# A seven-product FFN in layer 0 as well, and layer 1's conditioning dots in halves

## The chip, the cores and the metric

The kernel runs on one core of a Trainium2 chip. The metric is the device time of one execution in microseconds; the kernel before takes 2206.89 us (median of three runs, 2206.26 to 2207.37).

## What is computed

A trunk of two layers over 256 latent and 256 context tokens of width 1024. Each layer is a SwiGLU FFN of half weight, a token mixer (three kinds of attention, merged by gates) and a second such FFN. Every norm is modulated by a shift, a scale and a gate from a conditioning vector, one vector for the latent tokens and one for the context tokens. In layer 1 the context stream ends at the mixer.

```python
def _swiglu(h, w1, w3, w2):
    return (jax.nn.silu(h @ w1) * (h @ w3)) @ w2      # 1024 -> 2816 -> 1024

for l in range(DEPTH):                                # DEPTH = 2
    mx = jnp.split((sc_x @ ada_w[l] + ada_b[l])[:, None, :], N_MOD, axis=-1)   # N_MOD = 9
    mc = jnp.split(sc_c @ ada_w[l] + ada_b[l], N_MOD, axis=-1)
    x = x + mx[2] * 0.5 * _swiglu(_modulate(x, norm_gain[l, 0], mx[0], mx[1]), ...)
    xc = xc + mc[2] * 0.5 * _swiglu(...)
    y_x, y_c = _token_mixer(...)                      # with mx[3], mx[4], mc[3], mc[4]
    x = x + mx[5] * y_x
    x = x + mx[8] * 0.5 * _swiglu(_modulate(x, norm_gain[l, 2], mx[6], mx[7]), ...)
    if ctx_out:                                       # not in the last layer
        xc = xc + mc[5] * y_c
        xc = xc + mc[8] * 0.5 * _swiglu(...)
```

The conditioning vectors sc_x and sc_c go through a matrix of 1024 by 9216 for each layer. The kernel computes these nine modulation rows as dot products on VectorE: for each modulation m and each block k of 128 rows a load of 128 by 1024 (512 KB), and one dot with the vector of each stream that is needed.

## The kernel before

Activations lie with the features on the partitions, 512 tokens side by side (the first 256 latent, the other 256 context). Every weight and activation is split in two parts of a rounded format, hi and lo, and each product is three matmuls (`mm3`, L214 to L216): lo by hi, hi by lo, hi by hi. A weight unit is loaded by SP's queue, cast to hi on ScalarE and subtracted to lo on VectorE.

**A plain FFN** (the loop at L807) makes 22 tiles of 128 hidden features. A tile is two products with K = 1024 over 512 columns, a silu, a gate product, and a split into g. After groups of 8, 7 and 7 tiles comes an out phase: eight output blocks c, each accumulated over the group's tiles and added into x on VectorE. The layer's second FFN is (0, 1), the next layer's first is (1, 0).

**A seven-product FFN** (`ff_sevens`, L544), used for (1, 0) alone, takes two tiles as a 2 by 2 block matrix and saves one of eight block products. The token side uses combinations of the activations made once at the start (`token_forms`); the weight side is combined from the loaded blocks by two accumulating loads on GpSimd's queue (blocks n and s3) and two additions on VectorE (`preadd`, L594). The work is written out as a list of steps. For a pair p of tiles they are p2, p6, p5, p7, p1 of the next pair, p4, p3; each is 24 matmuls of 256 columns. After the pairs that end a group (6, 6 and 4 tiles; the last 6 are done by the ordinary out phase) come eight steps "out 0" to "out 7", each over the group's tiles with 512 columns. Out 0 leaves out the group's last two tiles; out 1 starts on the others, then does out 0's last two, then its own.

What a step's product needs is a form: the combined weight, cast by ScalarE to hi (L618) and subtracted by VectorE to lo (L627). There are four form buffers, so the form of step f + 4 is cast when step f is done. Loads go in the order of the steps through eight buffers of 128 by 1024 (`topup`, L578); a buffer is released when its form is made.

The order of ScalarE, VectorE, SP and GpSimd within `ff_sevens` is the written one (`manual_schedule`). After the matmuls of a step the loop writes: ScalarE's copy of the product's bank (s1, sv, sw or su; not in p2, p5 and p3), VectorE's low part of the previous gate result (L762), VectorE's sum with a second bank (p2, p7, p3) or, in an out step, the two additions into x (L722); then the cast and subtraction of form f + 4, and, in p2, p7, p4 and p3, the gate: silu on ScalarE, product on VectorE (L749), cast of g on ScalarE (L761). In p2, p7 and p3 the product is written behind the subtraction, in p4 ahead of it. The product banks q1 and q3 go on accumulating: p7 adds to q1 after ScalarE has copied sv, p4 after it has copied sw.

**The dots** of layer 1 (`ada`, L282) are a generator with two buffers of its own. In the plain FFN `hook` (L306) draws from it after every tile and out block; all 112 dots of layer 1 (five modulations for two streams, four for one) lie in (0, 1). Outside `ff_sevens` VectorE's order is set by a planner and not by the text.

Of the kernel before, what the change touches and what calls it, by code (L numbers as in the profile page):

```python
# [13 lines left out]
BF16 = mybir.dt.bfloat16  # L14
AF = mybir.ActivationFunctionType
ALU = mybir.AluOpType
# [4 lines left out]
KD = 8  # L21
# [9 lines left out]
STRASSEN = ((1, 0),)  # L31
# [47 lines left out]
class Builder:  # L79
# [6 lines left out]
    def __init__(self, ctx, tc, a):  # L86
# [21 lines left out]
        self.owed = 0.0  # L108

# [171 lines left out]

    def ada(self, l, mods, cond):  # L282
        nc, a = self.nc, self.a
        M, sm = self.mods[l], self.sm[l]
        self.araw = [self.qkv.tile([128, 1024], F32, tag="pair", name="araw") for _ in range(2)]
        for m in mods:
            ns = (0,) if l == DEPTH - 1 and m > 4 else (0, 1)
            for k in range(KD):
                raw = self.araw[k % 2]
                nc.sync.dma_start(raw, a["ada"][l, m, k])  # L290
                self.ada_dot(l, m, k, raw, cond, ns)
                if k < KD - 1:
                    yield len(ns)
            for s in ns:
                d = M[:, s, m, :]
                nc.vector.tensor_tensor(out=d, in0=d, in1=sm[:, SM_ADAB + m * KD:SM_ADAB + (m + 1) * KD], op=ALU.add)
                if m in (1, 4, 7):
                    j = m // 3
                    nc.vector.scalar_tensor_tensor(out=self.gs[l][:, s, j, :], in0=d, scalar=1.0,
                                                   in1=sm[:, SM_GAIN + j * KD:SM_GAIN + (j + 1) * KD],  # L300
                                                   op0=ALU.add, op1=ALU.mult)
                elif m in (2, 5, 8):
                    nc.vector.tensor_scalar_mul(d, d, 0.5)
            yield len(ns)
# [239 lines left out]
    def ff_sevens(self, l, i, banks, halves, gm):  # L544
# [20 lines left out]
        for p, k in steps:  # L565
# [3 lines left out]
            elif k in need:  # L569
                b = {"r0": (0, None), "r1": (1, None), "n": (2, 3), "s3": (0, 2), "r3": (3, None)}[need[k]]  # L570
                loads.append(((p, need[k]), W[p, b[0]], None if b[1] is None else W[p, b[1]], 1024))
        loads = deque(loads)
        free = deque(self.rawp.tile([128, 1024], F32, tag="raw", name="raw") for _ in range(4))
# [50 lines left out]
        def subs(new):  # L624
# [5 lines left out]
            preadd(state["nf"])  # L630
            topup()
# [133 lines left out]
        if pend[0]:  # L765
            pend[0]()
        return gts
# [829 lines left out]
    def build(self):  # L1597
# [8 lines left out]
        for l in range(DEPTH):  # L1606
# [10 lines left out]
                       lambda *v: self.start_norm(l, 2, acc2, *v), pre)  # L1617
            if not last:
                self.adaq = self.ada(l + 1, range(NMOD), self.cond(nc.scalar))
# [143 lines left out]
```

## Time and profile before

| | |
|---|---|
| median of 3 runs | 2206.89 us |
| profiled execution | 2206.14 us |
| its span, first to last instruction | 2204.4 us |
| TensorE busy | 2186.8 us, 99% |
| VectorE busy | 1543.9 us, 70% |
| ScalarE busy | 994.2 us, 45% |
| DMA, mean rate | 149 GB/s |
| granted TensorE clock | 0.999 |

In the rows PE is TensorE, PEld its weight load, DVE VectorE, ACT ScalarE, POOL GpSimd, SPq and POOLq the DMA queues of SyncE and GpSimd. Times are in microseconds from the start of the span, unless a mean in ns is named. A timeline's row is start, duration, engine, line, operation, written tile <- read tiles, shapes, count, and in brackets the idle time of the engine just before, with what ended it. Durations on VectorE, ScalarE and TensorE overlap the next instruction's start by some 0.1 us or more, so the cost in a full queue is read from start to start.

### The profile page before, as it was taken

The page shows a single profiled execution, that of the slowest core. Times are in us where ns is not written, and L with a number is a line of the kernel's source. Part 1 is how long each engine was busy: PE and PEld are TensorE (multiplying, and loading weights), DVE is VectorE, ACT ScalarE, POOL GpSimd, SP SyncE. Part 2 cuts the span into 40 slices and gives each one's busy share as a digit, 9 for nine tenths or more (in the row PEclk, how much of TensorE's full clock was granted, in tenths as well). Part 3 has the DMA queues.
Part 4 walks back from the last instruction along what each step waited for, and adds up shares of the span by engine and source line. Part 5 has one row for each costly group of instructions (what it writes and reads, how often), then busy time and mean ns, then how long its engine had stood idle before and what let it go on. Part 6 is the DMA issues. An engine that isn't in the chain of part 4 may idle for free.

```text
span 2204.4 us, 34597 instructions
## 1 busy us (share of the span) xinstructions
PE 2186.8 (99%) x12912; PEld 1901.0 (86%) x12912; DVE 1543.9 (70%) x3477; ACT 994.2 (45%) x2506; POOL 126.3 (6%) x162
## 2 busy tenths in 40 slices
PE   9999999999999999999999999999999999999998
PEld 6888888887888877888888899999998889889998
DVE  4787877759554455689787777666777776677665
ACT  4423233548443365433223345444554565565543
POOL 3000000101001000000000000000011101000000
PEclk9999999999999999999999999999999999999999
DMA  8565654222123212446568645654542233445553
GB/s 328 191 213 176 213 194 174 91 86 71 62 66 103 92 58 82 139 159 222 183 198 276 229 119 139 163 147 124 159 149 96 84 118 109 160 133 174 183 183 114
DMA packets 94808, 328.57 MB, mean 149 GB/s; under 512 B 10928, under 2 KB 11824, under 8 KB 94640
## 3 DMA queue, kind: packets, MB, share of 16 engines
q1 hardware_dynamic: 89280, 308.52, 42.5%
q0 software_dynamic: 4928, 16.78, 3.6%
q8 instruction: 102, 1.67, 0.3%
q10 hardware_dynamic: 432, 1.06, 0.2%
q14 instruction: 66, 0.54, 0.1%
HBM read 322.12 MB, written 4.19 MB: 148 GB/s over the span
## 4 chain that ended last, share of the span: by engine, by line
PE 85%; issue 9%; DVE 4%; ACT 1%; DMA 1%; POOL 0%; SPq 0%; POOLq 0%; DVEq 0%; ACTq 0%
PE mm L214 20%; PE mm L216 20%; PE mm L215 20%; PE s L215 5%; PE s L216 5%; PE s L214 5%; PE s L209 2%; PE o L209 2%; PE t L209 2%; PE t L1088 1%; DVE wlo L205 1%; DVE nm L1074 0%; PE t L865 0%; DVE wlo L627 0%; DVE P L1162 0%
## 5 line engine op out<-in xcount | busy, mean ns | idle before, releaser
L204 ACT CAST whi<-raw 128x256 fp32r<-128x256 f32 (+4 forms) x1246 | 463.6, 434 | 437.1 <-issue 197.1
L205 DVE TENSOR_TENSOR wlo<-raw,whi 128x256 fp32r<-128x256 f32 (+2 forms) x1238 | 508.2, 456 | 194.6 <-ACT whi L204 191.8
L214 PE MATMUL mm<-h,wlo 128*128 128x512 f32 (+2 forms) x1352 | 472.5, 349 | 0.0
L216 PE MATMUL mm<-h,whi 128*128 128x512 f32 (+2 forms) x1352 | 465.7, 344 | 0.0
L215 PE MATMUL mm<-h,whi 128*128 128x512 f32 (+2 forms) x1352 | 465.4, 344 | 0.0
L279 DVE SCALAR_TENSOR_TENSOR junk<-araw,cond 128x1024 bf16<-128x1024 f32 x224 | 270.9, 1219 | 22.8 <-DMA araw<-in_ada 22.4
L214 PEld LDWEIGHTS mm<-h,wlo 128*128 128x128 f32 (+1 forms) x1352 | 255.7, 189 | 35.2 <-issue 6.2
L216 PEld LDWEIGHTS mm<-h,whi 128*128 128x128 f32 (+1 forms) x1352 | 255.5, 189 | 31.4
L215 PEld LDWEIGHTS mm<-h,whi 128*128 128x128 f32 (+1 forms) x1352 | 255.8, 189 | 29.2 <-issue 0.2
L214 PE MATMUL mm<-g,wlo 128*128 128x512 f32 (+1 forms) x764 | 266.8, 349 | 0.0
L215 PE MATMUL mm<-g,whi 128*128 128x512 f32 (+1 forms) x764 | 265.9, 348 | 0.0
L216 PE MATMUL mm<-g,whi 128*128 128x512 f32 (+1 forms) x764 | 265.8, 348 | 0.0
L214 PE MATMUL s<-h,wlo 128*128 128x256 f32 (+1 forms) x768 | 252.2, 328 | 0.0
L215 PE MATMUL s<-h,whi 128*128 128x256 f32 (+1 forms) x768 | 252.2, 328 | 0.0
L216 PE MATMUL s<-h,whi 128*128 128x256 f32 (+1 forms) x768 | 252.1, 328 | 0.0
L214 PEld LDWEIGHTS mm<-g,wlo 128*128 128x128 f32 x764 | 144.6, 189 | 18.4
L215 PEld LDWEIGHTS mm<-g,whi 128*128 128x128 f32 x764 | 144.7, 189 | 18.2
L216 PEld LDWEIGHTS mm<-g,whi 128*128 128x128 f32 x764 | 144.6, 189 | 18.2
L215 PEld LDWEIGHTS s<-h,whi 128*128 128x128 f32 x768 | 146.0, 190 | 13.0
L214 PEld LDWEIGHTS s<-h,wlo 128*128 128x128 f32 x768 | 146.0, 190 | 13.0
L216 PEld LDWEIGHTS s<-h,whi 128*128 128x128 f32 x768 | 146.1, 190 | 12.8
L618 ACT CAST whi<-raw 128x1024 fp32r<-128x1024 f32 (+2 forms) x94 | 91.7, 975 | 93.3 <-PE mm L216 58.8
(304 smaller groups left out, 3345.4 us busy)
## 6 DMA issues: line engine op xcount, KB each, us to landing
raw<-in_w SPq DMA_DIRECT2D x130, 512.0 KB, 4.3
araw<-in_ada SPq DMA_DIRECT2D x128, 512.0 KB, 3.7
raw<-in_win SPq DMA_DIRECT2D x90, 512.0 KB, 3.3
raw<-in_w13p SPq DMA_DIRECT2D x50, 512.0 KB, 4.0
raw<-in_w2b SPq DMA_DIRECT2D x48, 448.0 KB, 3.9
raw<-in_w2a SPq DMA_DIRECT2D x24, 512.0 KB, 4.4
raw<-in_wbr SPq DMA_DIRECT2D x24, 512.0 KB, 3.3
raw<-in_w13p POOLq DMA_DIRECT2D x20, 512.0 KB, 5.6
```

The lines of the kernel that those rows point to most:

```text
L204: nc.scalar.copy(hi[:, c], raw[:, c])
L205: eng.tensor_tensor(out=lo[:, c], in0=raw[:, c], in1=hi[:, c].bitcast(F32), op=ALU.subtract)
L209: self.nc.tensor.matmul(out, lhsT=lhsT, rhs=rhs, start=start, stop=stop, **kw)
L214: nc.tensor.matmul(out, lhsT=sl, rhs=mh, start=start, stop=False, **kw)
L215: nc.tensor.matmul(out, lhsT=sh, rhs=ml, start=False, stop=False, **kw)
L216: nc.tensor.matmul(out, lhsT=sh, rhs=mh, start=False, stop=stop, **kw)
L279: self.nc.vector.scalar_tensor_tensor(out=junk, in0=raw, scalar=1.0, in1=cond[s], op0=ALU.mult, op1=ALU.mult, accum_out=self.mods[l][:, s, ...
L618: nc.scalar.copy(hi[:, :n], raws[key][:, :n])
L1088: nc.tensor.transpose(pt[:, b * 128:(b + 1) * 128], P[:, b * 128:(b + 1) * 128], self.ident)
```

## The change

The list `STRASSEN` of seven-product FFNs becomes (0, 1) and (1, 0). The norm ahead of (0, 1) keeps its results for the token forms (`stash`).

The dots of layer 1 leave the generator. `ff_sevens` puts their loads into its own list of loads, each behind the load of the step it is tied to, through the same eight buffers. In (0, 1) modulations 0, 1 and 2 are tied to the 24 out steps, one load of 512 KB each, for both streams. In (1, 0) modulations 3 and 4 (16 loads, both streams) are spread over the 24 out steps, and modulations 5, 6 and 7 (24 loads, latent stream only) over the 27 steps p1, p4 and p5 of the pairs after the first. When the form of such a step has been subtracted (in `subs`), one waiting load is taken and its dots are written into VectorE's order at that place. Each dot of 1024 becomes two dots of 512, since the conditioning vectors are now kept in four tiles of 512 columns (`cond_halves`); the sums of the second halves are added at the end of a modulation. Modulation 8 stays with the generator and goes into the last FFN, (1, 1), which remains plain: eight loads, eight dots of 1024, and a second copy of the conditioning vectors for them.

```diff
--- before.py
+++ after.py
@@ -28,7 +28,8 @@
 FF_GROUPS = ((0, 8), (8, 15), (15, 22))
 NMOD = 9
 EPS = 1e-6
-STRASSEN = ((1, 0),)
+STRASSEN = ((0, 1), (1, 0))
+DOTS = {(0, 1): ((0, 1, 2), ()), (1, 0): ((3, 4), (5, 6, 7))}
 ST_GROUPS = ((0, 6), (6, 12), (12, 16), (16, 22))
 GRID_W = 64
 ROPE_BASE = 10000.0
@@ -106,6 +107,7 @@
         self.fillq = deque()
         self.adaq = iter(())
         self.owed = 0.0
+        self.second = {}
 
     def tick(self, ns):
         self.clock["pe"] += ns
@@ -279,9 +281,46 @@
             self.nc.vector.scalar_tensor_tensor(out=junk, in0=raw, scalar=1.0, in1=cond[s], op0=ALU.mult, op1=ALU.mult,
                                                 accum_out=self.mods[l][:, s, m, k:k + 1])
 
+    def cond_halves(self, queue):
+        out = []
+        for s in range(2):
+            ts = [self.tmp("P") for _ in range(2)]
+            for i, t in enumerate(ts):
+                queue.dma_start(t, self.a["cvec"][s, :, i * T:(i + 1) * T].to_broadcast([128, T]))
+                self.nc.scalar.activation(t, t, AF.Silu)
+            out.append(ts)
+        return out
+
+    def half_dots(self, l, m, k, raw, streams):
+        M, nc = self.mods[l], self.nc
+        if k == 0:
+            self.second[m] = self.small(2 * KD, "ah", 2)
+        for s in streams:
+            for i, o in ((0, M[:, s, m, k:k + 1]), (1, self.second[m][:, s * KD + k:s * KD + k + 1])):
+                junk = self.tmp("junk", BF16)
+                nc.vector.scalar_tensor_tensor(out=junk[:, :T], in0=raw[:, i * T:(i + 1) * T], scalar=1.0, in1=self.halves[s][i],
+                                               op0=ALU.mult, op1=ALU.mult, accum_out=o)
+        if k == KD - 1:
+            for s in streams:
+                d = M[:, s, m, :]
+                nc.vector.tensor_tensor(out=d, in0=d, in1=self.second[m][:, s * KD:(s + 1) * KD], op=ALU.add)
+            self.ada_end(l, m, streams)
+
...
     def ada(self, l, mods, cond):
         nc, a = self.nc, self.a
-        M, sm = self.mods[l], self.sm[l]
         self.araw = [self.qkv.tile([128, 1024], F32, tag="pair", name="araw") for _ in range(2)]
         for m in mods:
             ns = (0,) if l == DEPTH - 1 and m > 4 else (0, 1)
@@ -291,16 +330,7 @@
                 self.ada_dot(l, m, k, raw, cond, ns)
                 if k < KD - 1:
                     yield len(ns)
...
+            self.ada_end(l, m, ns)
             yield len(ns)
 
     def hook(self, n):
@@ -569,7 +599,29 @@
             elif k in need:
                 b = {"r0": (0, None), "r1": (1, None), "n": (2, 3), "s3": (0, 2), "r3": (3, None)}[need[k]]
                 loads.append(((p, need[k]), W[p, b[0]], None if b[1] is None else W[p, b[1]], 1024))
+        plain = [deque(), deque()]
+        for m in DOTS[l, i][0]:
+            plain[0].extend((m, k, (0, 1)) for k in range(KD))
+        for m in DOTS[l, i][1]:
+            plain[1].extend((m, k, (0,)) for k in range(KD))
+        forms_at = [n for n, (p, k) in enumerate(steps) if not isinstance(k, str)]
+        pairs_at = [n for n, (p, k) in enumerate(steps) if k in ("p5", "p4", "p1") and p > 1]
+        where = {}
+        for at, q in ((forms_at, plain[0]), (pairs_at, plain[1])):
+            q = list(q)
+            for n, d in enumerate(q):
+                where[at[n * len(at) // len(q)]] = d
+        both, loads = loads, []
+        f = 0
+        for n, (p, k) in enumerate(steps):
+            if not isinstance(k, str) or k in need:
+                loads.append(both[f])
+                f += 1
+            if n in where:
+                loads.append((where[n], a["ada"][1, where[n][0], where[n][1]], None, 1024))
         loads = deque(loads)
+        waiting = deque(where[n] for n in sorted(where))
+        due = [0]
         free = deque(self.rawp.tile([128, 1024], F32, tag="raw", name="raw") for _ in range(4))
         extra = 4
         raws, forms, used = {}, {}, {-1, -2}
@@ -628,6 +680,12 @@
                 if steps[f][1] not in ("p1", "p2", "p6"):
                     release(key)
             preadd(state["nf"])
+            due[0] += sum(f in where for f, _, _ in new)
+            if due[0] and waiting[0] in raws:
+                due[0] -= 1
+                d = waiting.popleft()
+                self.half_dots(1, *d[:2], raws[d], d[2])
+                release(d)
             topup()
 
         pend = [None]
@@ -764,6 +822,11 @@
                 between[f]()
         if pend[0]:
             pend[0]()
+        while waiting:
+            d = waiting.popleft()
+            self.half_dots(1, *d[:2], raws[d], d[2])
+            release(d)
+            topup()
         return gts
 
     def gated(self, f, gt, cols):
@@ -1614,9 +1677,11 @@
             acc2 = self.tmp("acc")
             first, pre = self.first_units(self.ff_units(l, 1))
             self.mixer(l, SEQ if last else T, nxt, spills[l], acc2,
-                       lambda *v: self.start_norm(l, 2, acc2, *v), pre)
-            if not last:
-                self.adaq = self.ada(l + 1, range(NMOD), self.cond(nc.scalar))
+                       lambda *v: self.start_norm(l, 2, acc2, *v, stash=not last), pre)
+            if last:
+                self.adaq = self.ada(l, (8,), self.cond(nc.scalar))
+            else:
+                self.halves = self.cond_halves(nc.scalar)
             acc = self.tmp("acc")
             nxt, pre = (None, None) if last else self.first_units(self.ff_units(l + 1, 0))
             if last:
```

In the parts left out, the code that ends a modulation (bias, gain, half) moves unchanged from `ada` into `ada_end`.

## Rows read from the trace of the kernel before

**Rows 1.** The page, part 1: busy time, share of the span, instructions.
```profile
PE 2186.8 (99%) x12912; PEld 1901.0 (86%) x12912; DVE 1543.9 (70%) x3477; ACT 994.2 (45%) x2506; POOL 126.3 (6%) x162
```

**Rows 2.** Waits of TensorE: waiter <- releaser: us in total, times, longest.
```profile
PE o L209 <- ACT on L1184: 2.1, 2, 1.4
...
PE mm L214 <- ACT sv L679: 1.2, 2, 0.9
```

**Rows 3.** Windows: length, busy (count) of PE, PEld, DVE, ACT, POOL; clock, DMA, GB/s.
```profile
933.49:1297.32 363.83, 363.83 (x1769) 308.26 (x1768) 284.67 (x611) 120.55 (x303) 2.50 (x3) 1.00 0.61 202
1297.32:1647.02 349.70, 348.54 (x2480) 329.29 (x2479) 246.88 (x391) 168.52 (x284) 22.32 (x29) 1.00 0.54 146
1399.20:1459.70 60.50, 60.50 (x505) 60.46 (x505) 43.60 (x57) 34.76 (x55) 2.55 (x3) 1.00 0.58 155
1459.70:1492.40 32.70, 32.70 (x146) 27.05 (x145) 17.35 (x28) 8.18 (x10) 2.56 (x3) 1.00 0.60 148
1532.70:1554.50 21.80, 21.80 (x98) 17.99 (x97) 15.17 (x26) 7.09 (x10) 2.56 (x3) 1.00 0.80 216
1997.00:2030.00 33.00, 33.00 (x279) 32.85 (x278) 22.16 (x60) 18.53 (x51) 0.72 (x1) 1.00 0.43 137
```

**Rows 4.** Timeline of PE: a stage's start, 117 matmuls, out 0, 117 matmuls.
```profile
1239.63 0.39 PE L215 MATMUL mm<-h,whi 128*128 128x512 f32 x1
...
1265.92 0.39 PE L214 MATMUL mm<-g,wlo 128*128 128x512 f32 x1
...
1297.32 0.28 PE L214 MATMUL mm<-h,wx 128*128 128x256 f32 x1
...
1459.72 0.40 PE L214 MATMUL mm<-g,wlo 128*128 128x512 f32 x1
...
1569.79 0.28 PE L215 MATMUL mm<-tf,whi 128*128 128x256 f32 x1
...
1583.71 0.28 PE L214 MATMUL mm<-tf,wlo 128*128 128x256 f32 x1
```

**Rows 5.** Timeline of DVE in (0, 1): two dots of 1024 behind each other.
```profile
1014.84 1.22 DVE L279 SCALAR_TENSOR_TENSOR junk<-araw,cond 128x1024 bf16<-128x1024 f32 x1
1015.98 0.08 DVE L279 DVE_READ_ACCUMULATOR junk<-araw,cond 128x1 f32 x1
1015.98 1.22 DVE L279 SCALAR_TENSOR_TENSOR junk<-araw,cond 128x1024 bf16<-128x1024 f32 x1
```

**Rows 6.** Groups of DVE by form: count | busy us, mean ns | idle before.
```profile
L722 DVE SCALAR_TENSOR_TENSOR x<-mm,mods,x 128x256 f32<-128x256 f32 x48 | 21.0, 479 | 34.1 <-PE mm L216 34.1
...
L1162 DVE SCALAR_TENSOR_TENSOR P<-P,c 128x512 f32<-128x512 f32 x16 | 11.9, 742 | 0.0
...
L690 DVE SCALAR_TENSOR_TENSOR sw<-sw,s 128x512 f32<-128x512 f32 x9 | 6.1, 680 | 0.0
...
L627 DVE TENSOR_TENSOR wlo<-raw,whi 128x512 fp32r<-128x512 f32 x8 | 5.4, 686 | 0.7 <-ACT whi L618 0.6
```

**Rows 7.** Timeline of DVE in (1, 0), around the second out group.
```profile
1453.06 0.95 DVE L627 TENSOR_TENSOR wlo<-raw,whi 128x768 fp32r<-128x768 f32 x1
1453.93 0.42 DVE L749 TENSOR_TENSOR sw<-sw 128x256 f32<-128x256 f32 x1
...
1462.56 0.43 DVE L762 TENSOR_TENSOR g<-sv,g 128x256 fp32r<-128x256 f32 x1 [0.47 <-ACT g L761]
```

**Rows 8.** Timeline of ACT in the same pair: cast of g, copy, casts.
```profile
1445.92 0.41 ACT L761 CAST g<-s 128x256 fp32r<-128x256 f32 x1 [1.07 <-DVE s L749]
1446.24 0.58 ACT L679 COPY sv<-mm 128x512 f32<-128x512 f32 x1
1446.71 1.04 ACT L618 CAST whi<-raw 128x1024 fp32r<-128x1024 f32 x1
...
1455.17 0.83 ACT L618 CAST whi<-raw 128x768 fp32r<-128x768 f32 x1
```

**Rows 9.** The page, part 6: KB of one issue, median us to landing.
```profile
raw<-in_w13p POOLq DMA_DIRECT2D x20, 512.0 KB, 5.6
```

More of the change, by code (lines that the diff above doesn't have):

```diff
@@ L280, in ada_dot, with ada_end @@
                                                 accum_out=self.mods[l][:, s, m, k:k + 1])
+    def cond_halves(self, queue):
[21 more added lines that the diff above has]
+            self.ada_end(l, m, streams)
+    def ada_end(self, l, m, ns):
+        nc, M, sm = self.nc, self.mods[l], self.sm[l]
+        for s in ns:
+            d = M[:, s, m, :]
+            nc.vector.tensor_tensor(out=d, in0=d, in1=sm[:, SM_ADAB + m * KD:SM_ADAB + (m + 1) * KD], op=ALU.add)
+            if m in (1, 4, 7):
+                j = m // 3
+                nc.vector.scalar_tensor_tensor(out=self.gs[l][:, s, j, :], in0=d, scalar=1.0,
+                                               in1=sm[:, SM_GAIN + j * KD:SM_GAIN + (j + 1) * KD],
+                                               op0=ALU.add, op1=ALU.mult)
+            elif m in (2, 5, 8):
+                nc.vector.tensor_scalar_mul(d, d, 0.5)
     def ada(self, l, mods, cond):
         nc, a = self.nc, self.a
-        M, sm = self.mods[l], self.sm[l]
         self.araw = [self.qkv.tile([128, 1024], F32, tag="pair", name="araw") for _ in range(2)]
@@ L293, in ada @@
                     yield len(ns)
[L294 to L303, printed above, removed]
+            self.ada_end(l, m, ns)
             yield len(ns)
```

## The prediction

> **What bounds the kernel now.** I read the page first: TensorE is busy 99% of the span, VectorE 70% [rows 1]. The list of waits then says how little TensorE ever waits: its largest entry is 2.1 us, the longest single wait near these stages 0.9 us [rows 2]. So the end moves in two ways only: by matmul time taken out, and by waits put in. VectorE's 70% is an average and is read stage by stage.
>
> The windows give both kinds of FFN side by side, cut at their first matmuls [rows 3, 4]. The second FFN of layer 0, plain, takes 363.8 us; the first FFN of layer 1, with seven products, takes 349.7 us on the same sizes. VectorE works 284.7 us in the first, 112 dots of 1024 among it, and 246.9 us in the second, which has no dots. Inside the second, VectorE has 43.6 us of work in three pairs (60.5 us), 17.4 in an out group of six tiles (32.7 us) and 15.2 in the one of four (21.8 us).
>
> **What the seven products save.** Matmuls start 0.2266 us apart at 512 columns and 0.1200 us apart at 256 (116 steps between the first and last row of each kind [rows 4]). A plain pair of tiles is 96 × 0.2266 = 21.75 us, a pair by products 7 × 24 × 0.12 = 20.16 us, so ten pairs save 15.9 us. The measured difference of the two stages, 363.8 − 349.7 = 14.1 us, holds the ends and the few waits too, and I take that.
>
> **What the dots cost on VectorE.** Two dots of 1024 start 1.14 us apart; the accumulator's read adds nothing [rows 5]. No row shows the half dot. From below it is half of that, 0.57 us. From above, the slowest three-operand form of 512 lasts 0.742 us, where another lasts 0.680 us [rows 6]; VectorE starts the next instruction some 0.08 us before the last one ends (1.22 against 1.14 for the dot), so 0.66 and 0.60. I take 0.605: the dot costs no more than a plain form of its size. A load with both streams is then 4 × 0.605 = 2.42 us (2 × 1.14 = 2.29 before), one with a single stream 1.21 us. The first stage gets 24 × 2.42 = 58 us, the second 16 × 2.42 + 24 × 1.21 = 68 us. In total both fit: 246.9 + 58 = 305 and 246.9 + 68 = 315 of 349.7 us. What decides is where they stand.
>
> [...] The durations agree that a part is fixed (0.680 us at 512 elements, 1.219 at 1024 [rows 5, 6]), but the next instruction starts before an instruction's end, so not all of it is paid in a queue that is full. [...]
>
> **Where they stand, first of the two stages.** ScalarE and VectorE run this stage in written order. A dot comes behind the subtraction of the form it is tied to, and forms are cast four steps ahead. So the dots of outs 0 to 3 run in the steps p7, p1, p4 and p3 of the pair before, which are 2.88 us long, and those of outs 4 to 7 in the iterations of outs 1, 1, 2 and 3. In p7 and p3 the dot even stands ahead of the gate's product, whose last result (the low part of g) the second half of out 1 needs.
>
> Walk it at the second out group [rows 7]. Out 0 starts at 1459.72 [rows 4]. Its matmuls on the four ready tiles and those of out 1 are 24, so TensorE wants that result at 1465.16; it came at 1462.99, 2.2 us early. Now put 2.42 us behind each subtraction. The one of out 0 ends at 1453.93, its dot at 1456.35, the product at 1456.7; ScalarE then casts g (0.4), copies s1 (0.5) and casts out 1 (0.84) [rows 8], to 1458.4. VectorE: subtraction and dot of out 1 to 1461.75, product and subtraction of out 2 to 1463.0, dot to 1465.4, low part and sum to 1466.3, subtraction of out 3 to 1467.2, dot to 1469.6, product, ScalarE's cast of g and the low part to 1470.9. Four dots are 9.7 us, and only 1.8 us of it fell into idle time. TensorE waits 1470.9 − 1465.16 = 5.8 us. In the outs VectorE then has 0.80 (two evacuations, 0.479 each less the overlap [rows 6]) + 0.88 + 2.42 = 4.1 us a step against 4.08 of TensorE, and it carries two dots into out 1; the bank of out 2 comes free 0.4 us late. **6.2 us a group, twice.**
>
> The third group has four tiles: subtractions of 0.60 (0.686 less the overlap [rows 6]), so the result lands 9.9 us after the last product, but it is wanted after 12 matmuls, 2.7 us: 7.2 us. Then each step is 0.80 + 0.60 + 2.42 = 3.8 us on VectorE against 2.72, and outs 4 to 7 wait for banks: 2.5 + 1.05 + 1.05 + 0.4 = 5.0 us. **12.2 us.** This stage: 2 × 6.2 + 12.2 = **24.6 us** of waits.
>
> **The second stage.** 16 such loads stand at outs 0, 1, 3, 4, 6, 7; 1, 2, 4, 5, 7; 0, 2, 3, 5, 6 of the three groups. By the same walk, with the missing dot taken off and 1.2 us for a pair's dot that precedes: 5.8 − 2.4 + 1.2 = 4.6; 5.8 − 4.8 + 1.2 = 2.2; 7.2 − 2.4 + 1.2 = 6.0 and 1.2 at its later outs: **14.0 us.** The 24 single-stream loads put 3 × 1.21 = 3.6 us into a pair, in p2, p6 and p4. VectorE's 14.5 us of work become 18.1, and twice a pair (after the gate products of p2 and p7) it must wait 1.7 us for ScalarE's cast of g, copy of a bank (0.5) and cast of the next form (1.04) [rows 7, 8], with about 1.1 us more at the others: 22.6 against 20.16 us. Each of the 8 loaded pairs could thus cost 2.5 us: from 0, if the out groups give all of it back, to 20. The first pair of each of the four groups starts level with TensorE and pays nothing; four pay: **10 us.** This stage: **24.0 us.**
>
> **The rest.** The loads stay 72, but 64 of them now go through the FFN's eight weight buffers on SP's queue, each holding one until its dot is done; the FFN (0, 1) also gets 20 accumulating loads on POOL's queue, 5.6 us each to landing [rows 9]. The second stage would move 146 GB/s + 40 × 0.524 MB / 350 us = 206 GB/s; the plain stage carries 202 without a wait [rows 3]. I take 0, and 34 us if a load were late by one landing in each of six groups. The eight dots of 1024 left for the last FFN are 9.2 us of VectorE, which is idle 10.8 us in its first 33 [rows 3]; two silus and two broadcasts ride along: 0, at most 3 us. The token forms that the first stage gains are in the 349.7.
>
> **Sum.** The profiled execution took 2206.1 us (span 2204.4, 1.7 around it), 0.8 below the median. 2206.1 − 14.1 + 24.6 + 24.0 = **2240.6, say 2241 us**. With the half dot at 0.57 the waits fall by some 5 us, at 0.66 they grow by 10: 2236 to 2251.
>
> **The rivals.** *The dots hide (faster).* VectorE has 103 us free in such a stage, more than 58 or 68, and forms are made four steps ahead. If the low part of g is late by less than the 2.2 us in hand, only the saving shows: 2206.1 − 14.1 = 2192. That takes dots of under 1 us a load; against it stands the walk.
>
> *The dots come later (no change).* A dot is only issued if its load has a buffer; were they all held back into the out steps, the two even groups would balance, the short one cost 8 × 1.1 − 4.5 = 4 us: 2206.1 − 14.1 + 2 × 4 + 10 = 2210. Against it: at p7 the eight buffers hold r0, three outs and their dots, by my count of loads and releases.
>
> [...]
>
> *Loads late.* + 34 as above: 2275.
>
> **How the numbers follow.** Forecast 0.53; hidden 0.08; later 0.08; clock 0.20; loads 0.07; unnamed 0.04. Range 2212 to 2265: it leaves out the hidden dots, the late loads and part of the "later" case. A measurement of this kernel tells about 0.2% (4.4 us) from no change: faster 0.09, same 0.07, slower 0.84.
>
> **What would show it.** Right: both stages near 374 us; TensorE's waits 5 to 7 us long at out 1 of each group, put down to VectorE's low part of g; shorter ones at p7 of the second stage, put down to ScalarE's copy sv; half dots 0.6 us apart. Wrong: a first stage near 350 us, half dots far from 0.6 us, waits for DMA, or dots standing in other steps.

## The result, and the profile after

The changed kernel takes 2281.65 us (median of four runs, 2281.09 to 2284.17) against 2206.57 us for the kernel before (now four runs, 2206.19 to 2207.37): a ratio of 1.0342, interval 1.0329 to 1.0355. It is 75 us slower, where 34 had been forecast, and lies 17 us above the range.

The windows of the changed kernel, cut at the first matmuls of each part (one profiled execution, as in all rows below; columns as in [rows 3]: length, busy time of PE, PEld, DVE, ACT, POOL, granted clock, DMA share, GB/s): the second FFN of layer 0, the first of layer 1, its mixer, its last FFN.

```profile
934.24:1319.35 385.11, 360.01 (x2481) 334.30 (x2479) 304.28 (x598) 168.20 (x283) 19.53 (x22) 0.96 0.59 164
1319.35:1708.47 389.12, 361.71 (x2481) 337.39 (x2479) 316.27 (x635) 168.03 (x285) 23.09 (x29) 0.97 0.63 185
1708.47:2071.29 362.82, 355.94 (x2433) 317.49 (x2431) 263.78 (x712) 209.55 (x593) 37.53 (x52) 0.99 0.38 123
2071.29:2279.56 208.27, 195.61 (x1611) 194.93 (x1609) 133.66 (x325) 97.97 (x269) 0.70 (x1) 0.97 0.53 172
```

The last two parts of the kernel before:

```profile
1647.02:2003.92 356.90, 352.49 (x2432) 314.20 (x2431) 263.58 (x712) 206.26 (x590) 37.52 (x52) 1.00 0.37 122
2003.92:2204.37 200.45, 193.25 (x1611) 192.78 (x1609) 124.48 (x307) 99.45 (x270) 0.70 (x1) 0.99 0.49 158
```

Against [rows 3] the 75 us are: +21.3 in the second FFN of layer 0 (363.8 before), +39.4 in the first of layer 1 (349.7), +5.9 in the mixer, +7.8 in the last FFN, and 0.8 ahead of them. Both stages now have seven products, and 348.5 us of matmuls at the full clock; their busy time is 360.0 and 361.7, because the clock is granted at 0.96 and 0.97.

The waits of TensorE in the two stages (us in total, times, longest; first layer 0's, then layer 1's), where [rows 2] had at most 2.1 us in the whole span:

```profile
PE mm L216 <- ACT g L819: 18.7, 3, 6.8
PE mm L216 <- DVE x L780: 5.0, 5, 2.5
PE mm L216 <- ACT sv L737: 1.2, 2, 0.9
...
PE mm L216 <- ACT sv L737: 13.7, 7, 3.5
PE mm L216 <- ACT g L819: 10.7, 3, 6.0
PE mm L216 <- DVE x L780: 3.0, 3, 1.6
```

They sum to 24.9 and 27.4 us. In layer 0's stage they all fall in the three out groups but for 1.2 us. The windows of the six out groups (six, six and four tiles; layer 0's first) show where the time of the stages went:

```profile
1003.47:1046.79 43.32, 36.22 (x146) 28.62 (x145) 36.14 (x90) 10.38 (x15) 2.54 (x3) 0.88 0.66 195
1107.26:1149.75 42.49, 36.59 (x146) 28.58 (x145) 35.19 (x91) 8.77 (x12) 2.38 (x3) 0.92 0.65 189
1190.06:1226.89 36.83, 25.89 (x98) 19.83 (x97) 32.17 (x89) 7.29 (x11) 1.70 (x2) 0.86 0.69 206
1393.41:1432.30 38.89, 34.82 (x146) 28.12 (x145) 32.24 (x74) 10.09 (x14) 1.70 (x2) 0.96 0.64 191
1498.19:1532.57 34.38, 33.52 (x146) 26.88 (x145) 28.74 (x68) 8.37 (x11) 1.70 (x2) 1.00 0.67 194
1574.14:1608.26 34.12, 25.30 (x98) 19.45 (x97) 26.36 (x68) 8.19 (x13) 1.71 (x2) 0.90 0.65 185
```

An out group of six took 32.7 us, the one of four 21.8 [rows 3]. In layer 0's stage the groups are 10.6, 9.8 and 15.0 us longer. That sum, 35.4 us, is the whole of 385.1 less the 349.7 of a stage without dots. VectorE is busy for 36.1, 35.2 and 32.2 us there: more than TensorE's own 32.7, 32.7 and 21.8. In layer 1's stage the groups are 6.2, 1.7 and 12.3 us longer, and some 19 us stand in the product steps.

One wait, seen from both sides. TensorE at out 1 of the first group:

```profile
1008.71 0.39 PE L218 MATMUL mm<-g,whi 128*128 128x512 f32 x1
1015.90 0.79 PE L216 MATMUL mm<-g,wlo 128*128 128x512 f32 x1 [6.80 <-ACT g L819]
...
1016.96 0.63 PE L218 MATMUL mm<-g,whi 128*128 128x512 f32 x1
1017.38 0.63 PE L216 MATMUL mm<-g,wlo 128*128 128x512 f32 x1
```

and VectorE ahead of it, with ScalarE's cast of g (the second row from below):

```profile
1004.64 0.69 DVE L301 SCALAR_TENSOR_TENSOR junk<-raw,P 128x512 bf16<-128x512 f32 x1
...
1005.25 0.69 DVE L301 SCALAR_TENSOR_TENSOR junk<-raw,P 128x512 bf16<-128x512 f32 x1
...
1008.29 0.68 DVE L301 SCALAR_TENSOR_TENSOR junk<-raw,P 128x512 bf16<-128x512 f32 x1
...
1012.55 0.68 DVE L301 SCALAR_TENSOR_TENSOR junk<-raw,P 128x512 bf16<-128x512 f32 x1
...
1015.45 0.41 ACT L819 CAST g<-sv 128x256 fp32r<-128x256 f32 x1 [3.24 <-DVE sv L807]
...
1015.88 0.43 DVE L820 TENSOR_TENSOR g<-sv,g 128x256 fp32r<-128x256 f32 x1 [0.47 <-ACT g L819]
```

Here is the walk of the prediction: half dots 0.61 us apart, four loads of them, one behind each form's subtraction, and the gate's product behind the last. ScalarE's cast of g waits 3.24 us for that product. The cast is what ends TensorE's wait: it ends at 1015.86, and the next matmul, which multiplies wlo with the high part of g, starts at 1015.90. The low part of g, at 1015.88, starts only then. Behind the wait, matmuls start 0.43 us apart (1016.96 to 1021.22 in ten steps) instead of 0.2266 [rows 4]: the granted clock is 0.50 there, and 0.88 over the group. Before, it was 1.00 in every such window.

### The profile page after: what moved, and what is told of

It reads as the page before. It is cut to its first block, busy times and chain, and to the rows that moved or that the text cites. A ratio compares the mean times of both kernels' runs of the same rounds, so it can differ in the third digit from the quotient of the medians.

```text
span 2279.6 us, 36448 instructions
## 1 busy us (share of the span) xinstructions
PE 2202.7 (97%) x13623; PEld 1941.1 (85%) x13623; DVE 1643.2 (72%) x3727; ACT 1044.3 (46%) x2493; POOL 145.0 (6%) x182
## 4 chain that ended last, share of the span: by engine, by line
PE 67%; DVE 14%; issue 11%; ACT 4%; DMA 3%; POOL 0%; POOLq 0%; DVEq 0%; ACTq 0%
PE mm L216 17%; PE mm L217 16%; PE mm L218 16%; DVE wlo L679 4%; DVE junk L301 3%; PE s L218 3%; PE s L217 3%; PE s L216 3%; PE s L211 2%; PE o L211 2%; ACT whi L670 2%; DMA raw<-in_w13p 2%; PE t L211 2%; PE t L1151 1%; PE mm L211 1%
## 5 line engine op out<-in xcount | busy, mean ns | idle before, releaser
L207 DVE TENSOR_TENSOR wlo<-raw,whi 128x256 fp32r<-128x256 f32 (+3 forms) x1038 | 428.6, 458 | 183.0 <-ACT whi L206 180.6
L206 ACT CAST whi<-raw 128x256 fp32r<-128x256 f32 (+4 forms) x1046 | 390.0, 434 | 314.3 <-PE mm L218 135.2
L216 PE MATMUL mm<-h,wlo 128*128 128x256 f32 (+2 forms) x1272 | 433.1, 341 | 0.0
L218 PE MATMUL mm<-h,whi 128*128 128x256 f32 (+2 forms) x1272 | 426.1, 335 | 0.0
L217 PE MATMUL mm<-h,whi 128*128 128x256 f32 (+2 forms) x1272 | 425.9, 335 | 0.0
L670 ACT CAST whi<-raw 128x1024 fp32r<-128x1024 f32 (+2 forms) x188 | 183.0, 975 | 206.8 <-PE mm L218 108.5
L216 PEld LDWEIGHTS mm<-h,wlo 128*128 128x128 f32 (+1 forms) x1272 | 241.3, 190 | 28.9 <-issue 6.2
L218 PEld LDWEIGHTS mm<-h,whi 128*128 128x128 f32 (+1 forms) x1272 | 241.0, 189 | 25.2
L217 PEld LDWEIGHTS mm<-h,whi 128*128 128x128 f32 (+1 forms) x1272 | 241.4, 190 | 23.0 <-issue 0.2
L679 DVE TENSOR_TENSOR wlo<-raw,whi 128x1024 fp32r<-128x1024 f32 (+2 forms) x188 | 212.4, 1131 | 59.9 <-ACT whi L670 59.5
L216 PEld LDWEIGHTS s<-h,wlo 128*128 128x128 f32 x848 | 163.1, 192 | 11.6 <-DVE gg L509 4.7
L217 PEld LDWEIGHTS s<-h,whi 128*128 128x128 f32 x848 | 163.1, 192 | 6.9
L218 PEld LDWEIGHTS s<-h,whi 128*128 128x128 f32 x848 | 163.0, 192 | 6.6
```

The source lines that it names most:

```text
L206: nc.scalar.copy(hi[:, c], raw[:, c])
L207: eng.tensor_tensor(out=lo[:, c], in0=raw[:, c], in1=hi[:, c].bitcast(F32), op=ALU.subtract)
L216: nc.tensor.matmul(out, lhsT=sl, rhs=mh, start=start, stop=False, **kw)
L217: nc.tensor.matmul(out, lhsT=sh, rhs=ml, start=False, stop=False, **kw)
L218: nc.tensor.matmul(out, lhsT=sh, rhs=mh, start=False, stop=stop, **kw)
L670: nc.scalar.copy(hi[:, :n], raws[key][:, :n])
```

## The experiments

### Taking the dots, the loads, or both away

`e1` has an empty `DOTS`. `e2` keeps the loads:

```diff
-        for s in streams:
...
-                nc.vector.scalar_tensor_tensor(out=junk[:, :T], in0=raw[:, i * T:(i + 1) * T], scalar=1.0, in1=self.halves[s][i],
+        nc.vector.scalar_tensor_tensor(out=junk[:, :32], in0=raw[:, :32], scalar=1.0, in1=self.halves[0][0][:, :32],
```

`e6` keeps the dots (a weight's load has a key of two, a dot's one of three):

```diff
-                nc.sync.dma_start(b[:, :n], src)
+                if len(key) == 2:
+                    nc.sync.dma_start(b[:, :n], src)
...
-                nc.vector.scalar_tensor_tensor(out=junk[:, :T], in0=raw[:, i * T:(i + 1) * T], scalar=1.0, in1=self.halves[s][i],
+                nc.vector.scalar_tensor_tensor(out=junk[:, :T], in0=self.halves[1 - s][i], scalar=1.0, in1=self.halves[s][i],
```

> Layer 1's modulations 0 to 7 are left out here (their 64 loads and all their half dots; constants stand in their place); modulation 8 stays in the last FFN. Theory (VectorE's half dots stand ahead of work that TensorE waits for, and the granted clock falls after the longer waits): both seven-product stages run like the one of the kernel before, 349.7 us each, against 385.1 and 389.1, so 2281.7 - 35.4 - 39.4 = 2207 us, between 2202 and 2211, with the clock at 1.00 in both and the last FFN still some 14 us dear. Rival (the seven-product scheme itself costs what was lost in the second FFN of layer 0): that stage stays above 375 us and the time above 2230.

> All 64 loads of layer 1's conditioning matrix go through the buffers in their places, but each load's two or four half dots are replaced by one dot over 32 columns, so that the dots' sums are left out and the wait for each load stays. Theory (the time of the dots on VectorE makes the waits): as the run without dots and loads, 2207 us, between 2203 and 2214. Rival (the loads, their buffers and their queue make the waits): the waits for g at out step 1 and for sv stay near 52 us and the time stays above 2260.

> All 208 half dots stay in their places, but they read the two tiles of the condition instead of a load, and the transfers of the 64 loads are left out (their buffers are still taken and given back at the same places), so that layer 1's modulations are wrong. Theory (VectorE's time makes the waits; where the loads alone cost 18 us, the dots hide that): 2270 to 2283. Rival (dots and loads add up): 18 us less than with both, 2260 to 2266.

| run | us | ratio to before | layer 0's stage | layer 1's stage |
|---|---|---|---|---|
| neither (e1) | 2209.86 | 1.0005 to 1.0023 | 349.7 | 350.8 |
| loads only (e2) | 2228.28 | 1.0081 to 1.0115 | 357.9 | 360.8 |
| dots only, buffers still taken (e6) | 2279.92 | 1.0315 to 1.0350 | 384.8 | 385.9 |
| both (the change) | 2281.65 | 1.0329 to 1.0355 | 385.1 | 389.1 |

Stages of e1, with the clock back at 1.00:

```profile
934.11:1283.83 349.72, 348.58 (x2481) 329.33 (x2479) 246.41 (x390) 168.80 (x283) 19.50 (x22) 1.00 0.53 145
1283.83:1634.60 350.77, 348.65 (x2481) 329.33 (x2479) 247.73 (x393) 168.61 (x285) 23.04 (x29) 1.00 0.53 145
```

The seven products keep their promise: without dots the stage is 14.1 us shorter than the plain 363.8, as put. And e1 is still no faster than before, for its mixer and last FFN are 16 us dearer (below). Both theories of the loads missed in part. Alone the loads cost 18 us, which I had put at nothing; beside the dots their transfers add some 2 us (e6 still takes and gives back their buffers). The out group of four in e2, its wait on VectorE and its wait on TensorE:

```profile
1169.95:1199.99 30.04, 24.08 (x99) 19.25 (x97) 16.45 (x41) 6.99 (x10) 2.56 (x3) 0.89 0.85 252
```

```profile
DVE raw L647 <- DMA raw<-in_w13p: 6.9, 1, 6.9
...
PE mm L216 <- DVE x L775: 6.0, 1, 6.0
```

VectorE is busy only 16.5 us of 30.0. It stands 6.9 us before the sum for p6, whose accumulated load comes late, and the evacuations queued behind it keep a bank from TensorE. So two limits lie over each other in these groups: VectorE's dots, and behind them the weights' own loads. Whether the transfers or the taken buffers make those loads late, no run tells apart.

### Dots by place, and half of the dots

`e12` says which dots stay; the others are one dot over 32 columns, as in e2:

```diff
+        if stage == (0, 1) and m != 2 or stage == (1, 0) and m < 5:
+            return self.half_dots(1, m, k, raw, streams)
```

`e9`:

```diff
-            for i, o in ((0, M[:, s, m, k:k + 1]), (1, self.second[m][:, s * KD + k:s * KD + k + 1])):
+            for i, o in ((0, M[:, s, m, k:k + 1]),):
```

> Dots are left out by place, with all loads kept and one dot over 32 columns for each load whose half dots are gone: in layer 0's stage those of modulation 2 (its eight loads stand in the out group of four tiles), in layer 1's those of modulations 5 to 7 (24 loads, in the product steps). Theory: in layer 0's stage the first two out groups stay at 43 us and the third falls from 36.8 to the 30 us of the run of the loads alone, so the stage to about 378; in layer 1's the out groups keep their 20 us and the product steps lose most of their 18, so the stage falls to about 373: 2281.7 - 7 - 16 = 2259 us, between 2250 and 2266. Rival (a late VectorE in the products is what makes the out groups late): in layer 1's stage the out groups fall as well, and the stage to 362 or less.

> Each load keeps its place but only the first 512 of its 1024 products are summed: 104 half dots instead of 208, the second half of each sum is left out. Theory (room, not work, decides: an out group of six has 32.7 us of TensorE against 17.4 + 9.7 us of VectorE, so its dots now fit, an out group of four 21.8 against 15.2 + 9.7): layer 0's stage 357 to 362 us, layer 1's 360 to 366, near the run of the loads alone, and 2281.7 - 50 = 2232 us, between 2224 and 2240. Rival (each half dot costs its share): half of the 53 us between the run of the loads alone and the change, 2255.

`e12` took 2264.85 us (1.0246 to 1.0276), its stages 377.1 and 377.5. Its first and third out group in layer 0's stage, and the first in layer 1's (the third there takes 35.1 us):

```profile
1002.48:1045.36 42.88, 35.62 (x146) 28.19 (x145) 36.20 (x90) 10.38 (x15) 2.32 (x3) 0.92 0.65 195
...
1188.06:1217.91 29.85, 24.10 (x98) 19.28 (x97) 16.44 (x41) 6.99 (x10) 2.56 (x3) 0.89 0.84 252
1380.93:1419.78 38.85, 34.78 (x146) 28.10 (x145) 31.13 (x72) 10.11 (x14) 1.70 (x2) 0.96 0.65 189
```

This is as expected, place by place. Each group with dots keeps its length (42.9; 38.9, 35.1). The group whose dots are gone falls to the 30 us of the loads alone. The product steps of layer 1's stage lose some 14 of their 19 us when their dots go, and the out groups there do not get shorter by it: the costs are local. The time lies 6 us above the 2259 put, 4.5 us of it in layer 1's stage.

`e9` took 2247.78 us (1.0173 to 1.0203): 16 us more than expected, 7 less than half. Its stages are 367.6 and 372.0. The out groups of six come down to 36.4 and 34.2 us, and to 33.6 and 32.7 in layer 1's stage, near the 32.7 that their room says. The groups of four do not come near their 21.8 us; layer 0's takes 34.5, layer 1's 32.4:

```profile
1173.98:1208.50 34.52, 26.12 (x98) 19.99 (x97) 22.74 (x55) 6.99 (x10) 2.56 (x3) 0.85 0.78 226
```

There VectorE has 22.7 us of work but also waits 6.5 us for the same accumulated load as in e2. I had counted the dots' room and the loads' lateness as one or the other; in this group they add.

### Other places and another order

`e5` takes the dots out of `subs` and calls them at the end of a step:

```diff
-            if due[0] and waiting[0] in raws:
-                due[0] -= 1
...
+            dots()
             if f in between:
                 between[f]()
```

`e7` writes them one by one, so many a step (`i` is 1 in layer 0's stage, 0 in layer 1's):

```diff
+            dots(dots_of(p, k))
             new = casts()
...
+    if isinstance(k, str):
+        return 1 if i == 0 or k not in ("p3", "p7") else 0
+    return 0 if k < 2 else (4, 3, 0)[p] if i == 0 else (3, 4, 1)[p]
```

> Only the order is changed: each load's half dots are written at the end of their step, after the gate's product, instead of ahead of it behind the subtraction of the next form. Theory (the place in VectorE's order makes a good part of the waits): a walk along the written order with the durations of the trace gives 18 and 14 us of waits in the two stages instead of 25 and 26, so 2281.7 - 19 = 2263 us, and down to 2254 if the clock falls less often. Rival (the sum of VectorE's work, or the loads, sets the time, wherever the dots stand): 2276 or more.

> The same 64 loads and 208 half dots in the same two stages, and the same tail; but the half dots are written one by one over nearly all steps, instead of two or four together in the out steps and some product steps: in layer 0's stage one ahead of the subtraction in five of a pair's seven steps and 3, 4 or 1 in the out steps from the third on, in layer 1's one in each of the seven steps and 4, 3 or none in the out steps. Theory (the out groups cost what VectorE is asked there beyond its time: in the run of the change the three out groups of layer 0's stage are 10.6, 9.8 and 15.0 us longer than without dots, all of its 35.4): with that work spread over the stage the out groups fall back to some 34, 35 and 23 us, layer 0's stage to 362 and layer 1's, with more loads, to 370: 2281.7 - 23 - 19 = 2240 us, between 2228 and 2250. Rival (the sum of VectorE's work and of the loads in a stage decides, not its place): 2270 or more.

`e5` took 2284.47 us (1.0333 to 1.0364): the expected 19 us did not come. Layer 0's stage grew to 394.0, layer 1's fell to 381.6. In layer 0's the waits for g fell from 18.7 to 12.7 us (7.3 for ScalarE's cast, below, and 5.4 for the low part), but those for banks grew:

```profile
PE mm L216 <- DVE x L783: 16.2, 5, 7.2
PE mm L216 <- ACT g L822: 7.3, 3, 2.9
```

What VectorE is not asked ahead of out 1 it is asked ahead of the evacuations. With 35 us of work in 33 or 22 us of a group, this order inside the step only moved the wait. In layer 1's stage, whose groups ask less of VectorE, it gained 7.5 us.

`e7` took 2257.75 us (1.0216 to 1.0247), its stages 366.4 and 381.7. The same 208 half dots, 24 us cheaper by their places and those of their loads, and 18 short of what was expected. Layer 0's first and third out group:

```profile
1006.91:1039.60 32.69, 32.69 (x146) 27.03 (x145) 25.41 (x58) 8.18 (x10) 1.69 (x2) 1.00 0.64 183
...
1180.03:1206.51 26.48, 23.43 (x99) 18.93 (x97) 18.12 (x36) 6.99 (x10) 1.71 (x2) 0.94 0.64 179
```

The out groups of layer 0's stage cost 4.7 us instead of 35.4, but its product steps now cost 12, and those of layer 1's stage 25 instead of 19. Most of that are waits for ScalarE's copy sv (9.0 and 17.1 us in the two stages). So neither theory alone holds: the place decides much, and at 303 and 315 us of VectorE in such a stage no place that I tried was free.

### What the clock costs

In `e3` and `e3b` matmuls that nobody reads fill TensorE's waits; VectorE's work is untouched. The diff is that of e3b, without the fillings at the pairs; e3 has 6, 4, 6 and 3, 0, 5.

```diff
+        def warm(n):
+            for _ in range(n):
+                self.mm(self.o_bank(), self.ones, self.cb[:, 0:T])
+        out1 = {(0, 1): (4, 3, 4), (1, 0): (2, 0, 4)}[l, i]
...
                     run(1, w, range(ng - 2))
+                    warm(out1[p])
```

> Idle time of TensorE is filled with matmuls whose result nobody reads: 6, 4 and 6 ahead of the second part of out 1 in layer 0's stage, 3, 0 and 5 in layer 1's, two ahead of outs 3 and 4 in each four-tile group, and 1 to 3 ahead of the third product of five pairs in layer 1's stage; each takes some 0.85 us and waits for nothing. Nothing is taken from VectorE. Theory (the granted clock falls because TensorE stands idle in the longer waits): both stages are granted 1.00 instead of 0.96 and 0.97, and give back most of the 11.5 and 13.2 us by which their busy time exceeds 348.5 us; waits and filling matmuls together stay about 52 us, or some us more where a slow clock had covered for a late VectorE: 2281.7 - 24 = 2258 us, between 2254 and 2268. Rival (the clock falls for another reason, such as VectorE's load beside it): clock and time stay, 2278 or more.

> As the first run with filling matmuls, but fewer, so that each stretch of them (1.19 us apiece in that run's trace) ends before the wait that it fills: 4, 3 and 4 ahead of the second part of out 1 in layer 0's stage and 2, 0 and 4 in layer 1's, one ahead of out 3 in the four-tile groups, 1 or 2 ahead of the third product of pairs 1, 2, 5 and 9 in layer 1's stage. Theory A (the clock's fall costs the 11.5 and 13.2 us by which the busy time grew, on top of the waits): the first run lost its gain to fillings that overshot, and this one stands at 2257, between 2253 and 2262. Theory B (at the full clock TensorE only comes earlier to a VectorE that is late anyway, so the waits grow by most of what the clock gives back): 2266 to 2273, with the clock near 1.00 and waits plus fillings of some 28 and 34 us in the two stages.

`e3` took 2271.9 us (1.0280 to 1.0311), with 1.00 granted in both stages (378.6 and 385.1 us). `e3b` took 2275.98 (1.0298 to 1.0329). Both took longer than put, e3b longer than under either theory. Stages of e3, then of e3b, then the waits of e3b in layer 0's:

```profile
934.05:1312.61 378.56, 372.91 (x2521) 334.89 (x2519) 304.33 (x598) 168.27 (x283) 19.50 (x22) 1.00 0.60 167
1312.61:1697.71 385.10, 373.98 (x2525) 336.02 (x2523) 316.46 (x635) 167.76 (x285) 23.07 (x29) 1.00 0.65 187
...
933.32:1315.43 382.11, 367.99 (x2505) 334.56 (x2503) 304.36 (x598) 168.26 (x283) 19.54 (x22) 0.99 0.57 165
1315.43:1702.30 386.87, 367.03 (x2505) 335.26 (x2503) 315.99 (x635) 167.72 (x285) 23.07 (x29) 0.99 0.62 186
```

```profile
PE mm L216 <- ACT g L830: 6.7, 3, 2.4
PE mm L216 <- DVE x L788: 5.7, 7, 1.6
```

That idle time makes the clock fall is shown: with the waits filled it stays (1.00 in both stages of e3, against 0.96 and 0.97 in the change). But it was not worth 24 us. In e3b each stage has 12 fillings of 1.19 us, 14.3 us. Without them the busy time is 353.7 and 352.7, so 6.3 + 9.0 = 15 us of slow matmuls are gone, and the two stages are only 3.0 + 2.2 = 5.2 us shorter. The rest went into waiting: with another 1.2 us for sv, waits and fillings are 13.6 + 14.3 = 27.9 us in layer 0's stage, where the change has 24.9 us of waits. A faster TensorE mostly came earlier to a VectorE that was late anyway. That is the sum of theory B, waits and fillings of 28 and 34 us (27.9 and 34.1), though the time lies 3 us above its range. In e3, where the stages are granted 1.00, they are 6.5 + 4.0 us shorter: 10.6 us came back. A filling took 1.19 us where 0.85 had been put, so some may have overshot their wait, and the full worth of the clock could be more; no run shows how much.

### The tail

```diff
-                self.adaq = self.ada(l, (8,), self.cond(nc.scalar))
+                self.adaq = iter(())
```

> Modulation 8 of layer 1 is left out: its eight loads and dots in the last FFN and the second broadcast and Silu of the condition ahead of it (a constant stands in its place). Theory (these stand in ScalarE's and SP's queues ahead of the norm's and the first tiles' work, and make the waits of 2.8 and 4.5 us with a fall of the clock behind each): the mixer of layer 1 and the last FFN lose the 5.9 and 7.9 us that they gained, 2281.7 - 14 = 2268 us, between 2265 and 2271; the two stages stay. Rival (the dots cost nothing there, as the prediction had it, and the tail is longer for another reason): 2279 to 2283.

`e4` took 2265.86 us (1.0251 to 1.0282), 16 us less than the change by the medians, and 13 in these two parts of the profiled executions. Its mixer and last FFN are nearly as before, 356.5 and 201.4 us. The chain of waits of the changed kernel at the last norm (start, us):

```profile
2054.31 6.41 DMA cond<-in_cvec
...
2060.74 0.02 ACT cond L274
...
2061.70 0.41 ACT sq L353
```

The condition has two Silus, one for each stream. The second stands in ScalarE's queue ahead of the norm's last squares and waits there for its broadcast, which ScalarE issues only behind the first Silu and which takes 6.41 us. By the order of the code that is the vector of the context stream, which modulation 8 of layer 1 doesn't use: the norm also waits for a vector that no dot reads. Behind it the first tiles wait once more:

```profile
PE s L216 <- DVE gg L509: 4.5, 1, 4.5
PE t L211 <- DVE acc L354: 2.8, 1, 2.8
```

In that stretch VectorE's dots wait 4.5 us for their loads, and ScalarE 5.5 us for a weight load on the same queue of SP. That the dots as such cost next to nothing is shown by the next runs, which keep all eight.

### Fewer dots in the stages, and another order in the tail

`e8` and `e13` keep seven products in both stages. Modulations 0 and 5 of layer 1 go to layer 0's first FFN, each stage keeps 24 loads and 80 single half dots, and modulation 8 gets one broadcast and one Silu behind the first tiles of the last FFN. In e8 the first gates of that FFN were read before two of their eight dots and the bias.

```diff
+DOTS[_li] = [x for k in range(KD) for x in (_four[2 * k], _four[2 * k + 1], (_c, k, 1))]
...
-        self.adaq = self.ada(0, range(2, NMOD), cond)
+        self.adaq = chain(self.ada(0, range(2, NMOD), cond), self.ada(1, (0, 5), cond))
...
-                self.adaq = self.ada(l, (8,), self.cond(nc.scalar))
+                self.adaq = self.ada_late(l, 8)
```

> Both second FFNs stay with seven products. Layer 1's modulations 0 and 5 go to layer 0's first FFN (24 more whole dots there, its hooks raised from 2.2 and 0.9 to 2.8 and 1.15); each seven-product stage keeps 24 loads and 80 half dots (modulations 1, 2, 6 and 3, 4, 7), placed one by one: one ahead of the subtraction in four of a pair's seven steps, three, two or one in the out steps; modulation 8 stays in the last FFN, with one broadcast and one Silu behind its first tiles and one dot a hook. Theory (with room for each dot where it stands, and loads spread, neither waits nor falls of the clock remain): stages of 350 to 354 us and a tail as before, 2197 us, between 2191 and 2210. Rival (the loads keep the stages some 8 us long each, as in the run of the loads alone, and layer 0's first FFN is held up): 2212 to 2225.

> As the run with single dots and fewer of them in the stages, with modulation 8 of the last FFN done before its first use (there two of its dots came too late), the hooks of layer 0's first FFN at 2.95 and 0.9 (their out steps had VectorE too full: 9.7 us), and the first out groups lightened (two half dots a step instead of three, the others in product steps). Theory: layer 0's first FFN loses its 7.6 us of waits, the stages fall from 358.5 and 359.2 to 355 or 356: 2220.8 - 14 = 2207 us, between 2201 and 2213, about the kernel before. Rival (the 24 loads of each stage hold it up wherever the dots stand): the stages stay at 358 and the time at 2213 or more.

`e8` took 2220.78 us (1.0047 to 1.0077), `e13` 2231.81 (1.0099 to 1.0133); the rivals' times were right both times. Layer 0's first FFN with all ahead of it, the two stages, the mixer and the last FFN in e13:

```profile
0.00:406.42 406.42, 395.14 (x1884) 320.16 (x1884) 325.83 (x700) 135.99 (x326) 21.62 (x24) 0.99 0.65 225
947.96:1305.59 357.63, 350.05 (x2481) 329.30 (x2479) 293.56 (x564) 169.25 (x283) 19.54 (x22) 1.00 0.60 177
1305.59:1670.73 365.14, 353.58 (x2481) 332.23 (x2479) 295.04 (x566) 169.04 (x285) 23.07 (x29) 0.99 0.59 174
1670.73:2027.94 357.21, 352.74 (x2432) 314.33 (x2431) 263.52 (x712) 206.30 (x590) 37.53 (x52) 1.00 0.36 122
2027.94:2229.70 201.76, 193.27 (x1611) 192.79 (x1609) 132.78 (x325) 100.64 (x271) 0.70 (x1) 0.98 0.52 181
```

The tail is repaired with its dots in place (357.2 and 201.8). The stages are still 8 and 14 us above 350, and the 24 dots more in layer 0's first FFN hold that up by 14 us (its end lies at 392.5 in e1), where e8's even hooks had cost 10. None of these runs is faster than the kernel before.

## Why the prediction was wrong

The direction was right, and so was the cause of the waits, dots ahead of work that TensorE waits for. The size was not, and a sum of waits at the full clock was the wrong account of it. By its own steps:

- **What the products save:** right. 14.1 us put, 363.8 − 349.7 = 14.1 us in e1.
- **The half dot:** right. 0.605 us put, 0.61 between starts; VectorE 304.3 and 316.3 us in the stages, put at 305 and 315. The dots' durations, 0.685 us for 512 and 1.219 for 1024, leave 0.15 us of either as fixed (2 × 0.685 − 1.219). But an instruction behind another does not pay that in full: from start to start it is 0.61 and 1.14 us, which leaves 0.08.
- **The waits of layer 0's stage:** right in place and size, 24.6 us put and 24.9 measured; 6.8, 5.3 and 6.6 us at out 1, put at 5.8, 5.8 and 7.2. They end with ScalarE's cast of g, not with its low part as put. That the sum agrees so well is partly luck: it was put at the full clock and measured at a lower one (see the clock).
- **The waits of layer 1's stage:** 24.0 put, 27.4 measured. The out groups agree (14.0 put, 13.7), the pairs do not (10 put, 13.7), though they wait for ScalarE's copy sv, as put.
- **The clock:** this step failed. It stood as a rival with a chance of 0.20, the author's estimate, while the sum added its waits to matmuls at the full clock. TensorE's busy time grew by 11.5 + 13.2 = 24.7 us in the two stages: the granted clock is 1.00 in every window of [rows 3], and 0.86 to 0.96 in five of the six out groups after. The forecast thus missed the stages by 26.2 us: 24.7 of slow matmuls and 3.7 of waits, less the 1.2 us of waits a stage that the 349.7 held already. But e3 and e3b say that these 24.7 us are not the price of the clock. With all of them gone in e3, the stages fell by 10.6 us; waits took the place of the rest, so the walk was short as well. For a clock of 0.99 (e3b) it should have given 28 and 34 us of waits, fillings included, instead of 24.6 and 24.0. It had looked only at the steps around each wait, and left out what VectorE carries from one group into the next steps, and the late loads. Which of them made it short is not shown.
- **The tail:** this step failed. Put at 0, at most 3 us; the mixer and the last FFN grew by 13.7 us, and e4 gives that back. VectorE's idle time was the wrong row for it, and its window of 33 us even begins 6.9 us ahead of the last FFN's first matmul at 2003.92. The two broadcasts and Silus were named as riding along; their place in ScalarE's order ahead of the norm was not looked at, nor the loads between the weights on SP's queue.
- **The loads:** 0 put, and their transfers add some 2 us beside the dots (e6). But that was luck: alone the loads cost 18 us (e2).
- **The range:** with 26 + 14 us the two misses add to 40 of the 41 us. Its upper end lies 24 us above the forecast, which leaves no room for both.

The rivals of hidden and of later dots are out: the dots stand where the walk put them. The clock's rival was right in that the clock falls: layer 0's three out groups have 3.5, 3.9 and 4.1 us more matmul time than the 32.7, 32.7 and 21.8 before. But not all of that is added to the kernel's time (e3, e3b).

## What to carry over

Compare an engine's work with the other's time in each group of steps, not over a stage: 305 us fit into 350, and 36 did not fit into 33, nor 32 into 22. Even room is not enough where the order puts the work ahead of something that is waited for: layer 1's first out group, with 32.2 us of VectorE in 32.7, still cost 6.2 us. When a step is moved, cost every instruction that it issues in the queue where it lands, its broadcast and its activation too. And before a slow clock is blamed, ask who is late anyway: filling the idle time gave back 15 us of matmul time and 5 us of the kernel's (e3b).

## What was not expected of the hardware

A clock that falls in a wait cost less here than the slower matmuls behind it, as the engine that made the wait was late anyway: with 15 us of slow matmuls gone the stages were 5.2 us shorter (e3b), with all 24.7 gone 10.6 (e3, whose fillings take time of their own). The first out group of the changed kernel, by windows: the wait, the stretch behind it and the next.

```profile
1009.10:1015.90 6.80, 0.00 (x0) 0.00 (x0) 6.33 (x19) 0.82 (x2) 0.00 (x0) 0.67 0.73 227
1015.90:1026.20 10.30, 10.30 (x34) 8.19 (x35) 6.02 (x15) 2.12 (x3) 0.00 (x0) 0.72 0.30 94
1026.20:1036.00 9.80, 9.63 (x43) 7.61 (x42) 9.80 (x28) 2.27 (x3) 1.69 (x2) 1.00 0.85 241
```

TensorE stands still for 6.8 us. The granted clock of that stretch is 0.67 and of the 10.3 us behind it 0.72, both a mix of 1.00 and 0.50: it is 1.00 up to 1011.10, 0.50 from 1011.60 to 1021.50, and 1.00 again from 1022.00.

A weight load that is added onto another in its buffer takes a median of 7.1 us from issue to landing in the changed kernel, against 5.6 [rows 9]. It is 5.7 in e1, 7.0 in e2 and 6.9 in e6. So it grows with the loads alone, but also with the dots alone, where only buffers are taken and no transfer is added. Why, no run shows.
